# Down projections and the passage into the mixer of a trunk layer: the order of weight rounding, transposes and form sums

## The chip, the core and the metric

The kernel runs on one core of a Trainium2 chip. It is timed in device microseconds (us); the time before is 853.84 us, the median of three runs (853.50 to 854.26).

## What is computed

One layer of a decoder trunk, 512 tokens of width 1024, all in float32: a SwiGLU feed-forward network (FFN) of width 2816, a token mixer (pooling and sliding-window attention), and a second FFN, each between two RMS norms.

```python
def swiglu(h, w_gu, w_down):
    gate, up = jnp.split(h @ w_gu, 2, axis=-1)
    return (jax.nn.silu(gate) * up) @ w_down
...
h = swiglu(rms_norm(x, ffn1_pre[l]), ffn1_w_gu[l], ffn1_w_down[l])
x = x + 0.5 * rms_norm(h, ffn1_post[l])
h = token_mixer(rms_norm(x, mix_pre[l]), cos, sin, w_in[l], ...)
x = x + rms_norm(h, mix_post[l])
h = swiglu(rms_norm(x, ffn2_pre[l]), ffn2_w_gu[l], ffn2_w_down[l])
x = x + 0.5 * rms_norm(h, ffn2_post[l])
```

## The kernel before

**Matmuls in three.** A float32 product is made of three matmuls of a rounded kind: each operand is split into a high part (`hi`, rounded by a copy on ACT, L166 for weights, L630 for forms) and a low part (`lo`, the rest, a subtraction on DVE, L169 and L631). `mm3` (L356) issues hi by hi, hi by lo and lo by hi (L359 to L361).

**Weights.** The class `Weights` (L122) holds one list of weight tiles in the order of their use. `get(name, ahead)` makes all of them up to `ahead` beyond the one asked for (3 by default), `more(n)` the next n. For each one `make_to` (L153) issues loads on SP's queue, the rounding on ACT and the low part, on DVE or, where `W.lo` says so, on GpSimd (POOL). Six buffers of each part go round (WB), so the rounding of a tile waits until PE has used the tile six places before it, and a load waits until the low part of the tile whose raw buffer it takes is made. The order of rows on PE, DVE, ACT and POOL is the order of the code inside `in_order()`.

**The down projection** (`down_proj`, L611, once for each FFN) is a 2x2 block product of seven products, in the order 1, 5, 6, 3, 7, 2, 4. The 11 chunks of the hidden width go in pairs: weight tiles are named `d` with product and pair, so `f1_d70` to `f1_d75` are those of product 7 in the first FFN; the last, with one chunk, is half as wide. A pair is 12 matmuls, the last 6. The other operand is a *form* of the hidden activations (`form`, L617), three tiles for each product (`e70`, `e71`, `e72`), made during the product before it: products 5, 6, 3 and 7 first sum two tiles on DVE (L621 to L627), then ACT rounds and DVE makes the low part. Within a pair the weight is made first and the form behind it.

**Its end, and the passage.** When product 2 is over, `put_away(2)` (L665) adds it to what was kept. The tokens are four tiles of 128. Tiles 0 and 1 are complete then; tiles 2 and 3 are the two blocks that product 4 ends, one after the other (the tail: pairs 2 to 5, 21 matmuls for each block). For each tile ACT sums squares (`half_size`, L677), DVE applies the gain (`half_gain`, L686), `post_root` (L688) makes the mean square on DVE (L339) and its power on POOL (L334), and `add_to_x` (L691) updates x on DVE (L407). In the first FFN, steps of the mixer are woven into this by `then`: `size` (squares of x, L353), `root`, `norm` (xn, L378), `turn` (transposes on PE, L387; high parts xT on ACT, L393; low parts on DVE, L396) and `weights` (`weights1`, L906: the next tile of the mixer's input weights, wq0 to wq3, then wkv0, wkv1). The fourth of these and the first of wkv have their low part on POOL. PE then goes on in `mixer` (L1142) with `qkv_block(0)`: pq of tile 0 (24 matmuls of 512 columns), `turn1(2)`, pkv (24 of 256 columns), and a small transpose `pcols` before pq of tile 1. `root1(2)`, `norm1(2)`, `add_to_x(3)` and the rest of tiles 2 and 3 stand at the mixer's head.

Of the kernel before, what the change touches and what calls it, by code (L numbers as in the profile page):

```python
# [10 lines left out]
F32 = mybir.dt.float32  # L11
# [34 lines left out]
AHEAD = 3  # L46
# [21 lines left out]
def trunk_layer(  # L68
# [53 lines left out]
    class Weights:  # L122
# [25 lines left out]
        def split(self, name, shape):  # L148
            hi = wp.tile(list(shape), F32R, tag="hi", name=f"{name}_hi")
            lo = wp.tile(list(shape), F32R, tag="lo", name=f"{name}_lo")  # L150
            return hi, lo

        def make_to(self, n):  # L153
            while self.made < min(n, len(self.todo)):
                name, need, make, into = self.todo[self.made]
                self.load_to(need + self.run_ahead)
                src = make()
                if into is None:
                    hi, lo = self.split(name, src.shape)
                else:  # L160
                    whole, shape, at = into
                    if whole not in self.open:
                        self.open[whole] = self.split(whole, shape)
                    hi, lo = (part[at] for part in self.open[whole])
                if self.hi is nc.scalar:
                    nc.scalar.copy(hi, src)  # L166
                else:
                    nc.vector.tensor_copy(hi, src)
                self.lo.tensor_tensor(lo, src, hi.bitcast(F32), ALU.subtract)  # L169
                self.parts[name] = (hi, lo)  # L170
                self.made += 1

        def more(self, n):
            self.make_to(self.made + n)
# [436 lines left out]
    def down_proj(name, hs, ends, g_post, steps):  # L611
# [4 lines left out]

        def form(i, g):  # L617

            a11, a21, a12, a22 = (hs[g][:, f] for f in range(4))
            if i == 5:  # L620
                nc.vector.tensor_tensor(a21, a22, a21, ALU.subtract)  # L621
            elif i == 6:
                nc.vector.scalar_tensor_tensor(a11, a21, -1.0, a11, ALU.mult, ALU.subtract)  # L623
            elif i == 3:
                nc.vector.scalar_tensor_tensor(a21, a11, -1.0, a12, ALU.mult, ALU.subtract)  # L625
            elif i == 7:
                nc.vector.scalar_tensor_tensor(a11, a11, -1.0, a22, ALU.mult, ALU.subtract)  # L627
            src = {1: a11, 5: a21, 6: a11, 3: a21, 7: a11, 2: a12, 4: a22}[i]
            hi, lo = act_pair(f"{name}e{i}{g}", src.shape)
            nc.scalar.copy(hi, src)  # L630
            nc.vector.tensor_tensor(lo, src, hi.bitcast(F32), ALU.subtract)  # L631
            forms[i, g] = hi, lo
# [16 lines left out]
        def put_away(i):  # L649

            if i in (1, 5):
                kept[i] = wk.tile([P, 2, 512], F32, tag="sg2", bufs=2, name=f"{name}_p{i}")
                for t in range(2):
                    nc.scalar.copy(kept[i][:, t], into[i][t])
            elif i == 6:
                kept[i] = [slots_of["pool"].tile([P, 512], F32, tag="k", bufs=2, name=f"{name}_p6{t}") for t in range(2)]
                for t in range(2):
                    nc.scalar.copy(kept[i][t], xs_[t])
            for t in range(2):
                if i == 3:  # L660
                    nc.vector.scalar_tensor_tensor(kept[6][t], ys[t], -1.0, kept[6][t], ALU.mult, ALU.subtract)
                elif i == 7:
                    nc.vector.scalar_tensor_tensor(kept[5][:, t], xs_[t], -1.0, kept[5][:, t], ALU.mult, ALU.subtract)
                elif i == 2:
                    nc.vector.tensor_tensor(kept[1][:, t], zs_[t], kept[1][:, t], ALU.add)  # L665
# [28 lines left out]

        NW = (NCH + 1) // 2
        with behind(ends[0]):
            form(1, 0)
            form(1, 1)
        with behind(ends[1]):
            form(1, 2)  # L700
            W.get(f"{name}_d10")
        mix = steps if name == "f1" else {}

# [4 lines left out]
        with in_order():  # L708
            for at, i in enumerate(PRODUCTS[:-1]):
                for n in range(NW):  # L710
                    w = W.get(f"{name}_d{i}{n}")
                    if n % 2 == 0:
                        form(PRODUCTS[at + 1], n // 2)
                    multiply(i, n, w)
                    if n == 0 and at:
                        put_away(PRODUCTS[at - 1])
                    if i == 2 and 1 <= n <= 4:
                        half_size(n - 1, 1)
                        if n <= 2:
                            half_gain(n - 1, 1)  # L720
            i = PRODUCTS[-1]
            w = W.get(f"{name}_d{i}0")
            multiply(i, 0, w)
            put_away(2)
            for t in range(2):
                half_size(t, 0)
            for t in range(2):
                half_gain(t, 0)
                post_root(t)
            w = W.get(f"{name}_d{i}1")  # L730
            multiply(i, 1, w)
            for t in range(2):
                add_to_x(t)
                then("size", t)
            tail = [W.get(f"{name}_d{i}{n}", min(3, NW - 1 - n)) for n in range(2, NW)]
            then("root", 0)
            then("weights", 0)
            then("norm", 0)
            then("root", 1)
            then("weights", 1)  # L740
            then("norm", 1)
            for t in (2, 3):
                half_gain(t, 1)
            for n, w in enumerate(tail):
                multiply(i, n + 2, w, (0,))
            half_size(2, 0)
            half_gain(2, 0)
            post_root(2)
            for n, w in enumerate(tail):
                multiply(i, n + 2, w, (1,))  # L750
                if n == 1:
                    then("turn", 0)
                    then("weights", 2)
                    add_to_x(2)
# [82 lines left out]
    at = 0  # L837
# [65 lines left out]
            xT2.extend(act_pair(f"xT2_{i}") for i in range(4))  # L903
        transposes(t, xns[t], xT2, "mx")

    def weights1(n):  # L906
        W.run_ahead = 3
        W.lo = nc.gpsimd if n == 3 else nc.vector
        W.more(1)

    add_to_x = down_proj(
        "f1", hs, ends, g2,
        {"size": size1, "root": root1, "norm": norm1, "turn": turn1, "weights": weights1},
    )

    def project(ps, t, nm, per):
# [224 lines left out]

    def mixer():  # L1142
        with in_order():
            W.more(1)
            W.lo = nc.vector
            root1(2)
            norm1(2)
            add_to_x(3)
            W.more(1)
            size1(3)  # L1150
            qkv_block(0, lambda: turn1(2))
            root1(3)
            norm1(3)
# [232 lines left out]
```

## Time and profile before

| What | us |
|---|---|
| median of three runs | 853.84 |
| the profiled execution | 853.71 |
| its span on the core | 851.9 |
| mean granted TensorE clock over it | 0.989 of full |

The profile is of one execution. Engines: PE is TensorE (PEld its weight loads), DVE VectorE, ACT ScalarE, POOL GpSimd, SP the queue of loads. A row of a timeline has the start, the duration, the engine, the line, the operation, output and inputs, their shape and a count; in brackets stands how long the engine was idle ahead of it and what ended that. Names leave buffer numbers out, so `wq_lo` stands for the low part of any of the four. The view of waits has total time, number of times and longest. The granted clock is the share of full speed that TensorE was let run at.

### The profile page before, as it was taken

What the parts mean: (1) busy time and instruction counts of PE and PEld (TensorE: products, weight loads), DVE (VectorE), ACT (ScalarE), POOL (GpSimd) and SP (SyncE); (2) the same over time, 40 slices, a digit from 0 to 9 for tenths busy, and PEclk for the clock granted to TensorE, in tenths of its full rate; (3) what the DMA queues carried; (4) which work ended last, traced back from release to release, by engine and by line L of the source; (5) the groups of instructions that cost most, each with busy time, mean ns of one, the idle gap of its engine ahead of it and who ended that gap; (6) DMA issues with size and microseconds to landing.
All of it is one profiled execution on the core that took longest, in us unless ns stands there. A gap on an engine that the chain in (4) does not pass through costs nothing. (4 is left out here: it accounts for less than half of the span.)

```text
span 851.9 us, 14057 instructions
## 1 busy us (share of the span) xinstructions
PE 822.5 (97%) x5525; PEld 751.8 (88%) x5525; DVE 661.0 (78%) x854; ACT 467.5 (55%) x743; POOL 213.2 (25%) x293
## 2 busy tenths in 40 slices
PE   7999999999999999799999998999999999999996
PEld 5999999999988878688878878999999999888785
DVE  6987777777887799654666679777877778877895
ACT  6644445544555575535896567444444445555661
POOL 3103344433300001333532011133333344300001
PEclk9999999999999999989999999999999999999998
DMA  9428889988885567412005402268899888955542
GB/s 304 131 92 223 222 227 241 243 224 238 232 263 176 184 193 236 142 40 59 25 26 149 143 31 75 76 202 230 222 230 237 239 222 227 268 187 183 177 159 98
DMA packets 96877, 150.77 MB, mean 177 GB/s; under 512 B 6948, under 2 KB 53676, under 8 KB 96812
## 3 DMA queue, kind: packets, MB, share of 16 engines
q1 hardware_dynamic: 77100, 103.74, 38.0%
q0 software_dynamic: 19712, 46.15, 23.1%
q8 instruction: 43, 0.70, 0.3%
q14 instruction: 22, 0.18, 0.1%
HBM read 147.77 MB, written 48.23 MB: 230 GB/s over the span
## 5 line engine op out<-in xcount | busy, mean ns | idle before, releaser
L566 POOL DMA_DIRECT2D f_t<-in_ffn_w_down x132 | 89.6, 756 | 83.6 <-issue 50.7
L169 DVE TENSOR_TENSOR f_d_lo<-f_d_raw,f_d_hi 128x1024 fp32r<-128x1024 f32 x84 | 92.2, 1131 | 9.3 <-ACT f_d_hi L166 9.3
L166 ACT CAST f_d_hi<-f_d_raw 128x1024 fp32r<-128x1024 f32 x84 | 78.8, 977 | 6.9 <-PE f_z L361 6.7
L563 POOL COPY f_k<-f_h 1x1 f32<-1x1 f32 x18 | 21.0, 1166 | 130.8 <-DVE f_h L555 130.8
L590 ACT COPY f_h<-f_y 128x512 f32<-128x512 f32 x20 | 11.8, 588 | 76.1 <-PE f_y L361 75.5
L598 ACT ACTIVATE f_s<-f_s 128x1024 f32<-128x1024 f32 x20 | 21.2, 1061 | 41.5 <-DVE f_s L597 41.5
L566 POOL DMA_DIRECT2D f_t<-f_t x44 | 32.2, 795 | 36.6 <-issue 29.8
L630 ACT CAST f2e_hi<-f_h 128x1024 fp32r<-128x1024 f32 (+1 forms) x21 | 20.4, 977 | 30.9 <-DVE f_h L627 7.7
L630 ACT CAST f1e_hi<-f_h 128x1024 fp32r<-128x1024 f32 (+1 forms) x21 | 20.4, 977 | 30.7 <-DVE f_h L627 7.7
L595 ACT COPY f_s<-f_x 128x512 f32<-128x512 f32 x20 | 11.7, 587 | 46.3 <-PE f_x L361 46.3
L360 PE MATMUL f_x<-f_d_lo,f1e_hi 128*128 128x512 f32 x88 | 34.4, 390 | 0.8 <-DVE f_d_lo L169 0.8
L360 PE MATMUL f_x<-f_d_lo,f2e_hi 128*128 128x512 f32 x88 | 34.3, 390 | 0.8 <-DVE f_d_lo L169 0.8
L359 PE MATMUL f_x<-f_d_hi,f1e_hi 128*128 128x512 f32 x88 | 34.5, 392 | 0.7 <-DVE f_h L606 0.7
L359 PE MATMUL f_x<-f_d_hi,f2e_hi 128*128 128x512 f32 x88 | 34.4, 391 | 0.7 <-DVE f_h L606 0.7
L361 PE MATMUL f_x<-f_d_hi,f1e_lo 128*128 128x512 f32 x88 | 34.3, 389 | 0.0
L361 PE MATMUL f_x<-f_d_hi,f2e_lo 128*128 128x512 f32 x88 | 34.2, 389 | 0.0
L582 ACT COPY f_s<-f_x 128x512 f32<-128x512 f32 x20 | 11.7, 587 | 39.9 <-PE f_x L361 29.8
L631 DVE TENSOR_TENSOR f2e_lo<-f_h,f2e_hi 128x1024 fp32r<-128x1024 f32 (+1 forms) x21 | 23.6, 1133 | 11.4 <-ACT f2e_hi L630 11.4
L631 DVE TENSOR_TENSOR f1e_lo<-f_h,f1e_hi 128x1024 fp32r<-128x1024 f32 (+1 forms) x21 | 23.6, 1132 | 11.4 <-ACT f1e_hi L630 11.4
L334 POOL TENSOR_TENSOR r_f1po<-ms_f1po,half 128x1 f32<-128x1 f32 x4 | 3.5, 881 | 105.8 <-DVE ms_f1po L339 100.2
L334 POOL TENSOR_TENSOR r_f2po<-ms_f2po,half 128x1 f32<-128x1 f32 x4 | 3.5, 883 | 105.4 <-DVE ms_f2po L339 105.4
L359 PE MATMUL po<-wo_hi,yT_hi 128*128 128x512 f32 x64 | 25.3, 395 | 0.0
(1029 smaller groups left out, 3421.7 us busy)
## 6 DMA issues: line engine op xcount, KB each, us to landing
f_t<-in_ffn_w_down POOLq DMA_DIRECT2D x132, 256.0 KB, 6.3
f_d_raw<-f_t SPq DMA_DIRECT2D x40, 512.0 KB, 4.5
f_d_raw<-in_ffn_w_down SPq DMA_DIRECT2D x30, 512.0 KB, 4.4
f_t<-f_t POOLq DMA_DIRECT2D x44, 256.0 KB, 6.5
f_raw<-in_ffn_w_gu SPq DMA_DIRECT2D x8, 512.0 KB, 8.2
x<-in_x SPq DMA_DIRECT2D x4, 512.0 KB, 8.5
f_d_raw<-f_t SPq DMA_DIRECT2D x8, 256.0 KB, 3.7
wq_raw<-in_w_in SPq DMA_DIRECT2D x4, 512.0 KB, 4.2
```

The source lines that it names most:

```text
L166: nc.scalar.copy(hi, src)
L169: self.lo.tensor_tensor(lo, src, hi.bitcast(F32), ALU.subtract)
L359: nc.tensor.matmul(ps, wh, xh, start=first, stop=False, skip_group_check=open_)
L360: nc.tensor.matmul(ps, wh, xlo, start=False, stop=False, skip_group_check=open_)
L361: nc.tensor.matmul(ps, wlo, xh, start=False, stop=last, skip_group_check=open_)
L563: then = nc.gpsimd.tensor_copy(tick, hs[(c - 1) // 4][:1, 0, (c - 1) % 4, :1]).ins
L566: nc.gpsimd.dma_start(to, part, accum_op=op, max_dma_last_dim=2048)
L582: on_act.append(nc.scalar.copy(sg[:, :, a], px[:, :, a]).ins)
L590: on_act.append(nc.scalar.copy(h[1], py[:, :, a]).ins)
L598: on_act.append(nc.scalar.activation(sg, sg, AF.Silu, scale=-1.0).ins)
L630: nc.scalar.copy(hi, src)
L631: nc.vector.tensor_tensor(lo, src, hi.bitcast(F32), ALU.subtract)
```

## The change

`make_to` is cut in two: `begin` issues loads and the high part and returns what issues the low part. With it:
- the six input weights of the mixer are begun and ended at two places of the passage (`begin`, `low`), and all low parts are on DVE;
- the last product's weights are made earlier (`ahead` of 4 instead of 3 from the end of product 2 on, in both FFNs);
- both transposes of tiles 0 and 1 stand between the pairs of the tail's second block, at pairs 2 and 3; before, tile 0's stood behind pair 3 and tile 1's behind the block;
- the sums of squares of tile 2's x come behind the tail, the mean square of tiles 2 and 3 ahead of their gain (both FFNs);
- a form's sum stands ahead of the weight made in the same pair, its rounding and low part behind it (both FFNs).

```diff
+        def begin(self):
+            name, need, make, into = self.todo[self.made]
...
+            engine = self.lo
+            self.parts[name] = (hi, lo)
+            self.made += 1
+            return lambda: engine.tensor_tensor(lo, src, hi.bitcast(F32), ALU.subtract)
+
         def make_to(self, n):
             while self.made < min(n, len(self.todo)):
...
+                self.begin()()
...
             hi, lo = act_pair(f"{name}e{i}{g}", src.shape)
+            yield
             nc.scalar.copy(hi, src)
...
-                    w = W.get(f"{name}_d{i}{n}")
-                    if n % 2 == 0:
-                        form(PRODUCTS[at + 1], n // 2)
+                    half = form(PRODUCTS[at + 1], n // 2) if n % 2 == 0 else iter(())
+                    next(half, None)
+                    w = W.get(f"{name}_d{i}{n}", 4 if i == 2 and n == NW - 1 else AHEAD)
+                    next(half, None)
...
-            w = W.get(f"{name}_d{i}0")
+            w = W.get(f"{name}_d{i}0", 4)
             multiply(i, 0, w)
             put_away(2)
+            w = W.get(f"{name}_d{i}1", 4)
...
-            for t in range(2):
-                add_to_x(t)
-                then("size", t)
-            tail = [W.get(f"{name}_d{i}{n}", min(3, NW - 1 - n)) for n in range(2, NW)]
+            tail = [W.get(f"{name}_d{i}{n}", 0) for n in range(2, NW)]
+            then("begin", 0)
+            add_to_x(0)
+            then("size", 0)
+            add_to_x(1)
+            then("low", 0)
+            then("size", 1)
+            then("begin", 1)
             then("root", 0)
-            then("weights", 0)
+            half_gain(2, 1)
             then("norm", 0)
             then("root", 1)
-            then("weights", 1)
+            then("low", 1)
             then("norm", 1)
-            for t in (2, 3):
-                half_gain(t, 1)
+            half_gain(3, 1)
             for n, w in enumerate(tail):
                 multiply(i, n + 2, w, (0,))
             half_size(2, 0)
+            post_root(2)
             half_gain(2, 0)
-            post_root(2)
             for n, w in enumerate(tail):
                 multiply(i, n + 2, w, (1,))
+                if n == 0:
+                    then("begin", 2)
+                    then("low", 2)
+                    then("turn", 0)
                 if n == 1:
-                    then("turn", 0)
-                    then("weights", 2)
+                    then("begin", 3)
+                    then("low", 3)
                     add_to_x(2)
-                    then("size", 2)
+                    then("turn", 1)
+            then("begin", 4)
             half_size(3, 0)
+            then("size", 2)
+            then("low", 4)
+            post_root(3)
             half_gain(3, 0)
-            post_root(3)
-            then("turn", 1)
-            then("weights", 3)
...
-        W.lo = nc.gpsimd if n == 3 else nc.vector
-        W.more(1)
+        lows[n] = W.begin()
...
     def mixer():
         with in_order():
+            root1(2)
             W.more(1)
-            W.lo = nc.vector
-            root1(2)
             norm1(2)
             add_to_x(3)
-            W.more(1)
             size1(3)
```

Three places in the order of instructions. The first is DVE in the first FFN, during product 3, where the sums of product 7's forms (`h4`, `h8`: hidden activations) and the low parts of the weights stand. Before:

```order
L169 TENSOR_TENSOR f1_d34_lo_3347<-f1_d34_raw_3305,f1_d34_hi_3346 128x1024
L169 TENSOR_TENSOR f1_d35_lo_3365<-f1_d35_raw_3317,f1_d35_hi_3364 128x512
L627 SCALAR_TENSOR_TENSOR f1_h4_550<-f1_h4_550 128x1024
L631 TENSOR_TENSOR f1e71_lo_3370<-f1_h4_550,f1e71_hi_3369 128x1024
L169 TENSOR_TENSOR f1_d70_lo_3388<-f1_d70_raw_3344,f1_d70_hi_3387 128x1024
```

Now, from the sum on:

```order
L633 SCALAR_TENSOR_TENSOR f1_h4_550<-f1_h4_550 128x1024
L172 TENSOR_TENSOR f1_d35_lo_3368<-f1_d35_raw_3320,f1_d35_hi_3367 128x512
L638 TENSOR_TENSOR f1e71_lo_3364<-f1_h4_550,f1e71_hi_3363 128x1024
L172 TENSOR_TENSOR f1_d70_lo_3388<-f1_d70_raw_3344,f1_d70_hi_3387 128x1024
L633 SCALAR_TENSOR_TENSOR f1_h8_551<-f1_h8_551 128x768
```

The sum has gone ahead of one weight's low part; the form's own low part stays where it was.

The second is DVE in the passage, from the mean square of tile 0's x (`ms_b0`) to the norm of tile 2 (`xn_b2`); `f1_n2`, `f1_n3` and `f1_p5` are gains of tiles 2 and 3. Before, from tile 2's x on:

```order
L169 TENSOR_TENSOR wq2_lo_3852<-wq2_raw_3756,wq2_hi_3851 128x1024
L407 SCALAR_TENSOR_TENSOR x2_90<-f1_n2_3805,r_f1po2_3809,x2_90 128x512
L407 SCALAR_TENSOR_TENSOR x2_90<-f1_p5_3220,r_f1po2_3809,x2_90 128x512
L686 TENSOR_TENSOR f1_n3_3873<-f1_x1_2944,g2_2907 128x512
L339 SCALAR_TENSOR_TENSOR ms_f1po3_3875<-f1_sso_2945 128x1
L339 SCALAR_TENSOR_TENSOR ms_b2_3949<-ss2_b2_3857 128x1
L396 TENSOR_TENSOR xT2_0_lo_3824<-tr_mx10_3879,xT2_0_hi_3823 128x2x128
L396 TENSOR_TENSOR xT2_1_lo_3826<-tr_mx10_3879,xT2_1_hi_3825 128x2x128
L396 TENSOR_TENSOR xT2_2_lo_3828<-tr_mx11_3888,xT2_2_hi_3827 128x2x128
L396 TENSOR_TENSOR xT2_3_lo_3830<-tr_mx11_3888,xT2_3_hi_3829 128x2x128
L378 SCALAR_TENSOR_TENSOR xn_b2_3953<-x2_90,r_b2_3951,g3_2909 128x512 x2
```

Now, from the low part of wq3 on:

```order
L172 TENSOR_TENSOR wq3_lo_3858<-wq3_raw_3740,wq3_hi_3857 128x1024
L412 SCALAR_TENSOR_TENSOR x2_90<-f1_n2_3809,r_f1po2_3807,x2_90 128x512
L412 SCALAR_TENSOR_TENSOR x2_90<-f1_p5_3220,r_f1po2_3807,x2_90 128x512
L401 TENSOR_TENSOR xT2_0_lo_3824<-tr_mx10_3863,xT2_0_hi_3823 128x2x128
L401 TENSOR_TENSOR xT2_1_lo_3826<-tr_mx10_3863,xT2_1_hi_3825 128x2x128
L401 TENSOR_TENSOR xT2_2_lo_3828<-tr_mx11_3872,xT2_2_hi_3827 128x2x128
L401 TENSOR_TENSOR xT2_3_lo_3830<-tr_mx11_3872,xT2_3_hi_3829 128x2x128
L172 TENSOR_TENSOR wkv0_lo_3893<-wkv0_raw_3760,wkv0_hi_3892 128x1024
L344 SCALAR_TENSOR_TENSOR ms_f1po3_3903<-f1_sso_2945 128x1
L693 TENSOR_TENSOR f1_n3_3907<-f1_x1_2944,g2_2907 128x512
L344 SCALAR_TENSOR_TENSOR ms_b2_3949<-ss2_b2_3897 128x1
L172 TENSOR_TENSOR wkv1_lo_3956<-wkv1_raw_3817,wkv1_hi_3955 128x1024
```

Three low parts of weights (wq3, wkv0, wkv1) now stand on DVE ahead of `xn_b2`; before, none of them did, two of them being on POOL.

The third is PE in the tail's second block (`f1_x1`). Before, the last rows ahead of pq:

```order
L361 MATMUL f1_x1_2944<-f1_d43_hi_3682,f1e41_lo_3606 128x512
L387 MATMUL tr_mx00_3831<-ident_101,xn_b0_3764 128x128 x4
L387 MATMUL tr_mx01_3840<-ident_101,xn_b0_3764 128x128 x4
L359 MATMUL f1_x1_2944<-f1_d44_hi_3716,f1e42_hi_3650 128x512
L360 MATMUL f1_x1_2944<-f1_d44_lo_3717,f1e42_hi_3650 128x512
```

Now:

```order
L366 MATMUL f1_x1_2944<-f1_d42_hi_3670,f1e41_lo_3600 128x512
L392 MATMUL tr_mx00_3831<-ident_101,xn_b0_3770 128x128 x4
L392 MATMUL tr_mx01_3840<-ident_101,xn_b0_3770 128x128 x4
L364 MATMUL f1_x1_2944<-f1_d43_hi_3676,f1e41_hi_3599 128x512
L365 MATMUL f1_x1_2944<-f1_d43_lo_3677,f1e41_hi_3599 128x512
```

Tile 0's transposes have moved up by the six matmuls of pair 3; tile 1's, which before stood right ahead of pq, follow behind those six.

More of the change, by code (lines that the diff above doesn't have):

```diff
@@ L151, in split @@
             return hi, lo
+        def begin(self):
+            name, need, make, into = self.todo[self.made]
+            self.load_to(need + self.run_ahead)
+            src = make()
+            if into is None:
+                hi, lo = self.split(name, src.shape)
+            else:
+                whole, shape, at = into
+                if whole not in self.open:
+                    self.open[whole] = self.split(whole, shape)
+                hi, lo = (part[at] for part in self.open[whole])
+            if self.hi is nc.scalar:
+                nc.scalar.copy(hi, src)
+            else:
+                nc.vector.tensor_copy(hi, src)
+            engine = self.lo
+            self.parts[name] = (hi, lo)
+            self.made += 1
+            return lambda: engine.tensor_tensor(lo, src, hi.bitcast(F32), ALU.subtract)
         def make_to(self, n):
             while self.made < min(n, len(self.todo)):
[L155 to L171, printed above, removed]
+                self.begin()()
         def more(self, n):
@@ L696, in down_proj @@
         with behind(ends[0]):
-            form(1, 0)
-            form(1, 1)
+            for g in range(2):
+                list(form(1, g))
         with behind(ends[1]):
-            form(1, 2)
+            list(form(1, 2))
             W.get(f"{name}_d10")
@@ L729, in down_proj @@
                 post_root(t)
-            w = W.get(f"{name}_d{i}1")
             multiply(i, 1, w)
-            for t in range(2):
-                add_to_x(t)
-                then("size", t)
-            tail = [W.get(f"{name}_d{i}{n}", min(3, NW - 1 - n)) for n in range(2, NW)]
+            tail = [W.get(f"{name}_d{i}{n}", 0) for n in range(2, NW)]
[6 more added lines that the diff above has]
+            then("begin", 1)
             then("root", 0)
-            then("weights", 0)
+            half_gain(2, 1)
             then("norm", 0)
             then("root", 1)
-            then("weights", 1)
+            then("low", 1)
             then("norm", 1)
-            for t in (2, 3):
-                half_gain(t, 1)
+            half_gain(3, 1)
             for n, w in enumerate(tail):
@@ L904, in turn1, with begin1 @@
         transposes(t, xns[t], xT2, "mx")
-    def weights1(n):
+    lows = {}
+    def begin1(n):
         W.run_ahead = 3
-        W.lo = nc.gpsimd if n == 3 else nc.vector
-        W.more(1)
+        lows[n] = W.begin()
     add_to_x = down_proj(
         "f1", hs, ends, g2,
-        {"size": size1, "root": root1, "norm": norm1, "turn": turn1, "weights": weights1},
+        {"size": size1, "root": root1, "norm": norm1, "turn": turn1, "begin": begin1, "low": lambda n: lows[n]()},
     )
```

## The prediction

> **What bounds the kernel now.** I read the busy times first, then TensorE's waits by releaser, then the timeline of each engine round the longest of them, and last the granted clock there. This is the page's first part, busy us and share of the span:
>
> ```profile
> PE 822.5 (97%) x5525; PEld 751.8 (88%) x5525; DVE 661.0 (78%) x854; ACT 467.5 (55%) x743; POOL 213.2 (25%) x293
> ```
>
> TensorE (PE) is the bound, and the change leaves its instructions as many as they were. So only two things can be gained: time in which PE waits, and time in which its clock is low. The waits (us in total, times, longest) that lie where the change reaches:
>
> ```profile
> PE pq L359 <- ACT wq_hi L166: 3.2, 1, 3.2
> PE pq L360 <- POOL wq_lo L169: 1.9, 1, 1.9
> PE f_x L360 <- DVE f_d_lo L169: 1.7, 2, 0.8
> ...
> PE pt L1040 <- DVE st L1029: 1.0, 1, 1.0
> ```
>
> The first two lie in the passage from the first FFN to the mixer, the third once in each down projection; the last is the only one in the mixer behind the passage. PE's timeline of the passage (start, duration, what; in brackets the idle time ahead of a row):
>
> ```profile
> 346.80 1.03 PE L387 MATMUL tr_mx<-ident,xn_b 128*128 128x128 f32 x8
> 347.59 0.48 PE L359 MATMUL f_x<-f_d_hi,f1e_hi 128*128 128x512 f32 x1
> ...
> 354.48 0.39 PE L361 MATMUL pq<-wq_hi,xT_lo 128*128 128x512 f32 x1
> 358.07 0.50 PE L359 MATMUL pq<-wq_hi,xT_hi 128*128 128x512 f32 x1 [3.20 <-ACT wq_hi L166]
> 360.50 0.79 PE L360 MATMUL pq<-wq_lo,xT_hi 128*128 128x512 f32 x1 [1.93 <-POOL wq_lo L169]
> ...
> 364.12 1.97 PE L387 MATMUL tr_mx<-ident,xn_b 128*128 128x128 f32 x8 [1.12 <-DVE xn_b L378]
> ...
> 370.06 0.28 PE L359 MATMUL pkv<-wkv_hi,xT_hi 128*128 128x256 f32 x1
> 370.18 0.28 PE L360 MATMUL pkv<-wkv_lo,xT_hi 128*128 128x256 f32 x1
> ...
> 370.51 0.23 PE L1158 MATMUL pcols<-ident,rows 12*128 12x12 f32 x1
> ```
>
> Starts of 512-column matmuls stand 0.227 us apart where nothing waits, eight transposes take 0.79 (346.80 to 347.59), 256-column matmuls 0.12 (370.06 to 370.18). Between 354.71 (354.48 and 0.227) and 370.51 lie 6 of the first, 8 transposes and 24 of the last: 1.36 + 0.79 + 2.9 = 5.1 us of work in 15.8. So 10.7 us are lost, and the waits are only 6.3 of them. The rest is the clock. Stages of the trace with PE's busy time, granted clock, DMA share:
>
> ```profile
> 356.02:359.43 3.41, 0.50 (x1) 1.00 0.39 113
> 359.43:362.84 3.41, 2.34 (x5) 0.50 0.44 120
> ...
> 366.26:369.67 3.41, 3.41 (x18) 0.50 0.01 2
> 844.12:847.53 3.41, 0.84 (x4) 1.00 0.41 153
> ```
>
> The clock goes in steps of 3.41 us. After a step with one matmul it halves at 359.43, stays there through the half-filled step, and is back at 369.67, after the first full one. The step from 844.12, with 0.84 us busy, is followed by half clock too.
>
> **The form sums ahead of the low parts.** DVE, ACT and PE where product 7 of the first FFN begins:
>
> ```profile
> 299.32 1.22 DVE L627 SCALAR_TENSOR_TENSOR f_h<-f_h 128x1024 f32<-128x1024 f32 x1
> 301.66 1.23 DVE L631 TENSOR_TENSOR f1e_lo<-f_h,f1e_hi 128x1024 fp32r<-128x1024 f32 x1 [1.12 <-ACT f1e_hi L630]
> 302.80 1.22 DVE L169 TENSOR_TENSOR f_d_lo<-f_d_raw,f_d_hi 128x1024 fp32r<-128x1024 f32 x1
> ```
> ```profile
> 300.58 1.05 ACT L630 CAST f1e_hi<-f_h 128x1024 fp32r<-128x1024 f32 x1 [2.51 <-DVE f_h L627]
> ```
> ```profile
> 302.85 0.40 PE L359 MATMUL f_x<-f_d_hi,f1e_hi 128*128 128x512 f32 x1
> 304.07 0.50 PE L360 MATMUL f_x<-f_d_lo,f1e_hi 128*128 128x512 f32 x1 [0.83 <-DVE f_d_lo L169]
> ```
>
> DVE sums a form (1.14 us from start to start), ACT rounds it, DVE waits 1.12 for that, makes the form's low part, and only then the low part that PE wants at 304.07. With the sum first, DVE sums while ACT rounds the weights, and makes the weights' low part while ACT rounds the form. Up to product 7 each FFN has 10 sums that are moved so, about 1 us each, and DVE is ahead by far more than the 0.83 that was short. What is late next is the release of weight buffers, which is PE's own pace. The loss is 304.07 - 302.85 - 0.227 = 1.0, and about 0.1 in the next spacing; twice, **2.2 us**. Bounds: 0 if the load of that weight is what is late, 2.2 if all goes.
>
> **The end.** The root now precedes the gain. DVE and POOL after the last matmul:
>
> ```profile
> 845.78 0.69 DVE L686 TENSOR_TENSOR f_n<-f_x,g 128x512 f32<-128x512 f32 x1 [1.86 <-ACT j_f2po L677]
> 846.39 0.15 DVE L339 SCALAR_TENSOR_TENSOR ms_f2po<-f_sso 128x1 f32<-128x1 f32 x1
> 847.27 0.75 DVE L407 SCALAR_TENSOR_TENSOR x<-f_n,r_f2po,x 128x512 f32<-128x512 f32 x1 [0.73 <-POOL r_f2po L334]
> ```
>
> The mean square would start at 845.78 instead of 846.39, and the gain (0.61 to the next start) runs beside POOL's power: **0.6 us**, nothing behind it on DVE but the last sums.
>
> **The passage.** What sets its end in before: ACT's rounding of wq3 stands behind sums of squares that wait for x(2), POOL makes two low parts, and the root of tile 2 queues behind these.
>
> ```profile
> 330.00 1.06 ACT L166 CAST f_d_hi<-f_d_raw 128x1024 fp32r<-128x1024 f32 x1 [1.66 <-PE f_z L361]
> ...
> 353.79 0.63 ACT L353 ACTIVATE j_b<-x 128x512 bf16<-128x512 f32 x1 [4.21 <-DVE x L407]
> ```
> ```profile
> 345.86 1.40 POOL L334 TENSOR_TENSOR r_b<-ms_b,half 128x1 f32<-128x1 f32 x1 [2.26 <-DVE ms_b L339]
> ...
> 358.10 2.35 POOL L169 TENSOR_TENSOR wq_lo<-wq_raw,wq_hi 128x1024 fp32r<-128x1024 f32 x1 [0.62 <-ACT wq_hi L166]
> ...
> 362.73 0.55 POOL L334 TENSOR_TENSOR r_b<-ms_b,half 128x1 f32<-128x1 f32 x1
> ```
> ```profile
> 333.40 1.37 DVE L665 TENSOR_TENSOR f_p<-f_z,f_p 128x512 f32<-128x512 f32 x2 [0.72 <-PE f_z L361]
> ...
> 345.63 1.22 DVE L169 TENSOR_TENSOR wq_lo<-wq_raw,wq_hi 128x1024 fp32r<-128x1024 f32 x1
> ...
> 350.50 1.41 DVE L396 TENSOR_TENSOR xT_lo<-tr_mx,xT_hi 128x256 fp32r<-128x256 f32 x4
> ...
> 352.95 0.74 DVE L407 SCALAR_TENSOR_TENSOR x<-f_n,r_f1po,x 128x512 f32<-128x512 f32 x1
> ...
> 363.31 1.41 DVE L378 SCALAR_TENSOR_TENSOR xn_b<-x,r_b,g 128x512 f32<-128x512 f32 x2 [5.14 <-POOL r_b L334]
> ```
>
> Now DVE carries all of it in one queue, which I add up in before's clock times. A low part costs 1.14 from start to start (301.66 to 302.80), a half of xn 0.67 (1.41 for two, of which the second takes the 0.74 of a half), and so a half of x; a gain 0.61, a mean square 0.1, the four xT_lo 1.4. A root that POOL starts under a DVE operation on SBUF ends 0.5 after it (345.86: 1.40 instead of 0.55, to 0.5 behind the low part of 345.63).
> - d44's low part stands ahead of the product sums. Its high part waits for the buffer of d24, one weight tile (12 matmuls, 2.72) after the one released at 330.00: 332.7; ACT 1.06, DVE 1.22: 335.0. So the sums of 333.40 start at **335.0**. Two sums 1.37, d45's low part 0.6, two gains and a mean square 1.3, the root 0.5, four halves of x 2.7: 341.5.
> - wq0's low part, mean square, gain, root 0.5: 343.8; xn(0) to 345.2. Its transposes, six matmuls ahead of 346.80, stand at 345.4 on PE: no wait. wq1, root 0.5, xn(1): 348.3. PE wants its second half at 348.0 (345.4, 0.79, six matmuls, 0.4): 0.3 of waiting. Gain, mean square, gain, wq2, then xT_lo(0) from 350.7 to 352.0; pq, which now would start at 350.9 (17 spacings ahead of 354.48, and the 0.3), has the first of these at 351.1: another 0.3 at most.
> - wq3, x(2): 354.5 (before: 354.4). xT_lo(1), wkv0, mean square, gain, mean square, wkv1: 358.8; root 0.5; first half of xn(2) there at 360.1. Before: 364.05.
> - PE would end pq at 354.71 + 1.36 = 356.1, with the two waits 356.6. It then **waits 3.6 us** for the transposes of tile 2, which before waited for POOL. They start at 360.2, take 0.28 (second half) and 0.79, then 2.9 of pkv: pcols at 364.1 instead of 370.51, 6.35. The same sum on before's order comes out 0.15 early: **6.2 us**.
>
> ACT's part hides in this: it rounds wq3 as soon as PE has used d43, no longer behind the sums of squares of 353.79. SP's loads of wkv and wu come no later, as their buffers are those of d44, d45 and wq0, whose low parts DVE makes earlier or 1 us later. POOL loses two operations of 2.35 and 2.3, and DVE's 1.14 each stand in the sum.
>
> The clock: from 356.6 to 361.3 PE has no matmul but transposes. On a grid of 3.41, some step keeps at most (6.83 - 4.7) / 2 = 1.1 us of matmuls, near the 0.84 that was followed by half clock and far from the 2.3 that keep neither. So I let it halve, until the first full step: 3.4 to 6 us of work at half clock cost 1.7 to 3.0, and I take 2.3. The passage gives 6.2 - 2.3 = **3.9 us**.
>
> **A rule against this forecast.** This step had nothing but transposes (columns: PE, PEld, DVE, ACT, POOL, clock):
>
> ```profile
> 7.86:11.27 3.41, 1.24 (x10) 0.84 (x8) 2.78 (x6) 1.67 (x4) 0.55 (x1) 1.00 1.04 356
> ```
>
> The clock was half in the step behind it. The Trainium skill, "TensorE: Matmul & The Clock Gate", Part 4: PE-mode transpose, says that transposes do not count as busy; by that rule, the trace agrees. The same page, Part 1: The HAM clock gate, lets the clock fall after an idle window of about 3.4 us; the step at 356.02, with a matmul in it, speaks against reading this as wholly idle. By that reading the sum would be the first rival's.
>
> **Sum.** 853.71 for the profiled execution (its median 853.84 is 0.02% above), less 2.2, 0.6 and 3.9: **847.0 us**. Its own range, from a clock cost of 1.7 to 3.4, the first term at 1.7, and 0.7 in the sum of DVE's queue: 845.7 to 848.7.
>
> **Rivals.**
> - The clock stays at full, since no step of the grid is wholly without matmuls: a whole one fits into 4.7 us in 1.3 / 3.41 of all positions. Against it: 356.02 and 844.12. 853.71 - 2.2 - 0.6 - 6.2 = 844.7.
> - The form sums change nothing, because d70's load or buffer is what is late, not DVE's queue. For it speaks only that a load is not seen in that row; 847.0 + 2.2 = 849.2.
> - DVE's queue, without a gap from 335 to 360, is longer: some 45 operations at 0.03 more, and a second half-filled step at half clock (1.7): 850.
> - The passage's gain is given back by a wait further on in the mixer, and the forms bring nothing: 853.1. Against it: PE's one wait of 1.0 in the mixer behind the passage is for its own chain.
> - Slower: a sum of 1.14 ahead of a low part delays PE wherever that low part has no lead. It decides from four such sums (4.5 / 1.14, the forms' 2.2 being lost then) of the 22 that are moved. If the 18 of products 6, 3 and 7 all do, 849.2 + 20.5 = 869.7. Against it: DVE idles 1.12 behind the sum in the rows above.
>
> **Chances.** Forecast 0.52, full clock 0.20, longer queue 0.12, forms without effect 0.10, given back 0.03, slower 0.03. A measurement of this kernel tells 0.2% (1.7 us) from no change: faster 0.94, within 0.03, slower 0.03. From 844.3 to 850.2 the range takes in all but the last two.
>
> **What would show it.** The wait of 0.83 before f_d_lo gone in both FFNs; wq_hi and wq_lo gone from PE's waits; instead one wait of 3 to 4 us of tr_mx for xn_b, with half clock for one or two steps behind it; POOL with roots alone until wpl; the last mean square ahead of the gain. A wait of tr_mx under 2.5 us, or a clock that stays full, makes it too slow a forecast; a new wait for f_d_lo or put_away, too fast.

## The result, and the profile after

| | before | after |
|---|---|---|
| median, us (4 runs each, in turns) | 854.05 | 843.98 |
| lowest and highest | 853.50, 854.31 | 843.83, 844.82 |
| profiled execution, us | 853.71 | 843.83 |
| its span, us | 851.9 | 841.9 |

The ratio is 0.9883, 95% interval 0.9871 to 0.9895. The forecast was 847.0 with a range from 844.3: faster, but by 3 us more than forecast.

First the engines, from the page of the changed kernel (busy us, share of the span, instructions). TensorE's matmuls are as many as before, its share is the same 97%; what went is waiting, and some half clock:

```profile
PE 819.0 (97%) x5525; PEld 750.6 (89%) x5525; DVE 662.7 (79%) x856; ACT 470.1 (56%) x743; POOL 207.8 (25%) x291
```

PE's waits in the changed kernel where the prediction spoke of them (us in total, times, longest):

```profile
PE tr_mx L392 <- DVE xn_b L383: 3.5, 1, 3.5
...
PE f_x L364 <- DVE f_h L611: 1.4, 2, 0.7
...
PE pt L1057 <- DVE st L1046: 1.0, 1, 1.0
```

The waits of pq for `wq_hi` and `wq_lo` are gone, and so are both of `f_x` for `f_d_lo`; the new one of `tr_mx` is there with 3.5 (3.6 forecast). But the view of before has one more line that no longer appears, and the prediction did not name it:

```profile
PE f_x L359 <- DVE f_s L534: 1.6, 1, 1.6
```

It lies in the second FFN, 170 us behind the passage, where the first product of a gate and up pair (`f2_x1`) begins. PE and DVE's last `f_s` there, first in before, then in the changed kernel:

```profile
533.86 0.64 PE L478 MATMUL f_c<-f2b_lo,f_c_hi 128*128 128x256 f32 x4
536.14 0.36 PE L359 MATMUL f_x<-f2b_hi,f_1p_hi 128*128 128x256 f32 x1 [1.64 <-DVE f_s L534]
...
535.31 0.68 DVE L534 SCALAR_TENSOR_TENSOR f_s<-f_c,f_s 128x512 f32<-128x512 f32 x1
```
```profile
527.61 0.64 PE L483 MATMUL f_c<-f2b_lo,f_c_hi 128*128 128x256 f32 x4
528.09 0.28 PE L364 MATMUL f_x<-f2b_hi,f_1p_hi 128*128 128x256 f32 x1
...
529.07 0.67 DVE L539 SCALAR_TENSOR_TENSOR f_s<-f_c,f_s 128x512 f32<-128x512 f32 x1
```

In the changed kernel PE starts `f2_x1` before that `f_s`, in before behind it.

The passage in the changed kernel, PE's timeline and then DVE's:

```profile
344.35 1.03 PE L392 MATMUL tr_mx<-ident,xn_b 128*128 128x128 f32 x8
...
346.61 1.03 PE L392 MATMUL tr_mx<-ident,xn_b 128*128 128x128 f32 x8
...
354.76 0.39 PE L366 MATMUL pq<-wq_hi,xT_lo 128*128 128x512 f32 x1
358.69 1.58 PE L392 MATMUL tr_mx<-ident,xn_b 128*128 128x128 f32 x8 [3.54 <-DVE xn_b L383]
359.92 0.56 PE L364 MATMUL pkv<-wkv_hi,xT_hi 128*128 128x256 f32 x1
...
364.33 0.23 PE L1173 MATMUL pcols<-ident,rows 12*128 12x12 f32 x1
```
```profile
333.85 1.28 DVE L672 TENSOR_TENSOR f_p<-f_z,f_p 128x512 f32<-128x512 f32 x2
...
353.03 1.41 DVE L401 TENSOR_TENSOR xT_lo<-tr_mx,xT_hi 128x256 fp32r<-128x256 f32 x4
354.36 1.22 DVE L172 TENSOR_TENSOR wkv_lo<-wkv_raw,wkv_hi 128x1024 fp32r<-128x1024 f32 x1
...
356.22 1.22 DVE L172 TENSOR_TENSOR wkv_lo<-wkv_raw,wkv_hi 128x1024 fp32r<-128x1024 f32 x1
357.88 1.41 DVE L383 SCALAR_TENSOR_TENSOR xn_b<-x,r_b,g 128x512 f32<-128x512 f32 x2 [0.44 <-POOL r_b L339]
```

PE runs through both transposes and all of pq without a stop, then waits for DVE, whose queue is never idle for more than 0.44 from 333.85 to the norm of tile 2 at 357.88. The clock there, in stages with PE's busy time and the granted clock behind the engines' busy times:

```profile
352.78:356.19 3.41, 2.37 (x11) 1.63 (x9) 3.41 (x9) 1.21 (x4) 0.41 (x1) 1.00 0.40 154
356.19:359.60 3.41, 0.91 (x6) 0.67 (x7) 2.97 (x6) 0.00 (x0) 1.54 (x2) 1.00 0.51 154
359.60:363.02 3.42, 3.42 (x18) 3.42 (x17) 1.95 (x5) 2.94 (x10) 0.00 (x0) 0.50 0.01 2
```

One step of 3.41 us has no matmul but 0.91 us of transposes; the next one is at half clock, and full again behind it.

**Where the 10 us are.** Whole times carry a scatter that has nothing to do with the change: the first matmul of the first down projection starts anywhere from 241.4 to 243.6 in the fourteen traces of this case, though nothing ahead of it differs. So I cut each trace at five starts on PE and compare the stretches. In the changed kernel the first, the second and the fourth of these are:

```profile
242.03 0.40 PE L364 MATMUL f_x<-f_d_hi,f1e_hi 128*128 128x512 f32 x1
...
397.58 0.38 PE L1057 MATMUL pt<-ident,st 128*128 128x128 f32 x2
...
729.69 0.40 PE L364 MATMUL f_x<-f_d_hi,f2e_hi 128*128 128x512 f32 x1
```

The third is the `f_x` at 528.09 above, the fifth the last matmul (835.17). In before they start at 241.83, 403.78, 536.14, 737.79 and 844.58. Stretch A, from the first to the second, holds the first down projection, the passage and qkv; B the rest of the mixer up to `f2_x1`; C the second gate and up; D the second down projection; E the end. The differences of the starts, for all kernels that were run (us):

| kernel | A | B | C | D | E | bank of `f2_c11` |
|---|---|---|---|---|---|---|
| before | 161.95 | 132.36 | 201.65 | 106.79 | 7.35 | 1 |
| after | 155.55 | 130.51 | 201.60 | 105.48 | 6.73 | 5 |
| b_forms | 159.97 | 132.32 | 201.66 | 105.51 | 7.34 | 1 |
| b_turn1 | 162.24 | 130.60 | 201.60 | 106.80 | 7.34 | 6 |
| b_end | 161.83 | 132.33 | 201.67 | 106.84 | 6.75 | 1 |
| b_nopool | 159.48 | 132.33 | 201.66 | 106.80 | 7.35 | 1 |
| a_oldforms | 156.81 | 132.38 | 201.66 | 106.84 | 6.74 | 1 |
| a_turns_back | 155.49 | 130.48 | 201.60 | 105.48 | 6.74 | 5 |
| a_ahead_back | 153.24 | 132.35 | 201.66 | 105.49 | 6.75 | 1 |
| a_fill | 154.11 | 134.13 | 201.66 | 105.49 | 6.74 | 0 |
| a_pool | 156.25 | 132.31 | 201.66 | 105.51 | 6.74 | 1 |
| a_pool_early | 156.52 | 130.50 | 201.60 | 105.49 | 6.75 | 5 |
| a_norm_first | 153.03 | 133.22 | 201.66 | 105.50 | 6.74 | 1 |
| a_both_lows_late | 152.02 | 130.48 | 201.60 | 105.49 | 6.73 | 5 |

After against before: A 6.40 less, B 1.85, D 1.31, E 0.62, together 10.2; the changed kernel's first start is 0.2 later, so its span is 10.0 shorter. The last column is read from the built programs and is the key to B. PSUM, the memory into which TensorE writes its sums, is handed out by the kernel as eight banks or as four pairs of them: `f2_c11` is the fourth of the four gate and up tiles that stand ahead of `f2_x1`, and `f2_x1` takes PSUM banks 0 and 1 in every one of these programs.

### The profile page after: what moved, and what is told of

Its sections match the earlier page's. It is cut to its first block, busy times and chain, and to the rows that moved or that the text cites. A ratio compares the mean times of both kernels' runs of the same rounds, so it can differ in the third digit from the quotient of the medians.

```text
span 841.9 us, 14062 instructions
## 1 busy us (share of the span) xinstructions
PE 819.0 (97%) x5525; PEld 750.6 (89%) x5525; DVE 662.7 (79%) x856; ACT 470.1 (56%) x743; POOL 207.8 (25%) x291
## 5 line engine op out<-in xcount | busy, mean ns | idle before, releaser
L172 DVE TENSOR_TENSOR f_d_lo<-f_d_raw,f_d_hi 128x1024 fp32r<-128x1024 f32 x84 | 94.8, 1131 | 25.3 <-ACT f_d_hi L166 25.3
```

The lines of the kernel that those rows point to most:

```text
L172: return lambda: engine.tensor_tensor(lo, src, hi.bitcast(F32), ALU.subtract)
```

## The experiments

Names with b_ are the kernel before with one thing changed, names with a_ the changed kernel.

**b_forms: the form sums alone.**

```diff
             hi, lo = act_pair(f"{name}e{i}{g}", src.shape)
+            yield
...
-                    w = W.get(f"{name}_d{i}{n}")
-                    if n % 2 == 0:
-                        form(PRODUCTS[at + 1], n // 2)
+                    half = form(PRODUCTS[at + 1], n // 2) if n % 2 == 0 else iter(())
+                    next(half, None)
+                    w = W.get(f"{name}_d{i}{n}")
+                    next(half, None)
```


> The kernel before with the form sums moved and nothing else. If the forms' term holds: both waits of 0.8 us of f_x for f_d_lo gone, 2.2 us off, 851.8 us. If the release of weight buffers is what is late there: 854.0, with a wait of f_x for something else in their place. In both cases the wait of 1.6 us of f_x for f_s in the second FFN stays, since the last gate and up block (f2_c11) still has PSUM bank 1 there; if the form sums are what removed that wait, 850.0.

851.46 us against 853.71 beside it, ratio 0.9971 (0.9959 to 0.9982). Both waits for `f_d_lo` are gone, D is 1.28 less, and the wait for `f_s` stays. A is 1.98 less: 1.27 of it up to the last matmul of the first down projection, the rest in the passage, whose wait for `wq_lo` is 1.6 there in place of 1.9 and whose three steps of half clock end earlier in pkv. The release of weight buffers does not hold these places.

**b_turn1: one statement written earlier, for its bank.**

```diff
-            post_root(3)
             then("turn", 1)
+            post_root(3)
```


> The kernel before with the transposes of tile 1 written one statement earlier, ahead of tile 3's mean square; PE's order is the same, and in the built program f2_c11 comes to bank 6 instead of bank 1, which lies under the pair f2_x1. Theory of the bank: the wait of 1.6 us for f_s goes though nothing else changes, 1.8 us off, 852.1 us, and the passage takes what it took. Theory that the wait went because DVE reaches that place earlier in the changed kernel: the wait stays at 1.6, 853.9 us.

852.74 against 853.71, ratio 0.9990 (0.9981 to 0.9999). PE's order is the same instruction by instruction, except that the built program has one wait less, the one right ahead of `f2_x1`. A is 0.3 longer, which was not expected: on DVE the low parts of tile 1's xT now stand ahead of two mean squares, and the wait for `wq_lo` is 2.6 in place of 1.9. B falls by 1.76: the wait for `f_s` is gone. PE and DVE in this run:

```profile
534.32 0.28 PE L359 MATMUL f_x<-f2b_hi,f_1p_hi 128*128 128x256 f32 x1
```
```profile
535.28 0.68 DVE L534 SCALAR_TENSOR_TENSOR f_s<-f_c,f_s 128x512 f32<-128x512 f32 x1
```

DVE does its last `f_s` at the same place as in before (535.31), and PE no longer waits for it: that operation reads `f2_c11`, which is in bank 6 here and so not under `f2_x1`.

**a_oldforms: the changed kernel without the moved sums.**

```diff
-                    next(half, None)
                     w = W.get(f"{name}_d{i}{n}", 4 if i == 2 and n == NW - 1 else AHEAD)
-                    next(half, None)
+                    list(half)
```


> The changed kernel with each form's sum behind the weight's low part again. The two waits for f_d_lo come back (2.2 us). Theory of the bank: the built program has f2_c11 in bank 1 again, so the wait for f_s comes back too (1.85 us): 848.0 us. Theory of the passage (what DVE does there sets it): the wait stays away, 846.2 us.

848.69, ratio 0.9941 (0.9929 to 0.9953), against 0.9883 of the changed kernel. A and D are longer by 1.26 and 1.36, and B by 1.87, with the wait back although the passage is that of the changed kernel:

```profile
531.76 0.36 PE L364 MATMUL f_x<-f2b_hi,f_1p_hi 128*128 128x256 f32 x1 [1.64 <-DVE f_s L539]
```

So neither the forms nor the passage remove it as such; the bank does. In the table B is 130.5 or 130.6 in all five kernels with bank 5 or 6, and 132.3 or more in all nine with bank 0 or 1. The built programs also show where the bank is decided. The changed kernel and a_oldforms agree in every PSUM tile's bank up to the end of the mixer, and so do before and b_turn1 with each other. There `po111` and `po110`, two sums of the mixer's output projection, come to each other's banks, and `f2_c11` gets the bank that `po110` had. In the five kernels with bank 5 or 6 `po111` has bank 1; in the other nine it does not.

**b_end: the mean square ahead of the gain, second FFN only.**

```diff
             half_size(3, 0)
-            half_gain(3, 0)
+            if mix:
+                half_gain(3, 0)
             post_root(3)
+            if not mix:
+                half_gain(3, 0)
```
(and the same for tile 2.)


> The kernel before with the mean square of tiles 2 and 3 ahead of their gain in the second FFN only. If the end's term holds: 0.6 us less from the last matmul to the end, 853.4 us. If the root there waits for something else, 854.0.

853.53 against 853.71, ratio 0.9998 (0.9989 to 1.0007): as a whole time it can't be told from nothing. In the trace E is 0.60 less, which is the term.

**a_fill: work for PE in its wait.**

```diff
         project(pq, t, "wq", 2)
+        if t == 0:
+            pkv, wh = bank(f"pkv{t}"), W.get("wq3", 0)[0]
+            for _ in range(14):
+                nc.tensor.matmul(pkv, xT2[0][0][:, 0, :P], wh[:, 0], start=True, stop=True)
         between()
-        pkv = bank(f"pkv{t}")
+        if t:
+            pkv = bank(f"pkv{t}")
```


> The changed kernel with 14 more matmuls of 512 columns on PE between pq and the transposes of tile 2 (3.2 us, inside the wait of 3.5; their product is overwritten). Theory that the half clock comes from the step without matmuls: the wait shrinks to 0.4, the clock stays full, and from the first pq to the first pt PE needs 46.4 us in place of 48.0. Rival, that the half clock has another cause (the transposes, or what follows them): 48.0 still. The built program has f2_c11 in bank 0 under f2_x1, so the wait for f_s comes back by the theory of the bank (1.85): 844.2 us with the first, 845.8 with the second.

845.92, ratio 0.9903 (0.9888 to 0.9917). No half clock in the passage, a wait of 0.4, and A is 1.44 less; from the first pq to the first pt 46.6 (349.71 to 396.30) in place of 48.0. Two steps of its clock at the place where the changed kernel had 0.91 us of work and then half clock:

```profile
356.86:360.27 3.41, 2.95 (x18) 2.12 (x17) 2.96 (x5) 0.04 (x1) 1.16 (x1) 1.00 0.49 150
360.27:363.68 3.41, 3.41 (x27) 3.21 (x27) 1.94 (x6) 3.38 (x11) 0.00 (x0) 1.00 0.01 2
```

The transposes of tile 2 start as late as in the changed kernel (116.7 behind the first start in both). So the half clock cost 1.4 to 1.5, and what makes it in this place is the step without matmuls. The total did not follow, since B grew by 3.62: the wait for `f_s` (1.0 here), and two steps at half clock that the changed kernel's trace does not have. The forecast of 844.2 had counted neither of these two steps. The stages around both:

```profile
431.94:435.36 3.42, 2.46 (x18) 2.11 (x18) 1.51 (x6) 2.89 (x8) 0.61 (x1) 1.00 0.02 5
435.36:438.77 3.41, 3.41 (x9) 2.62 (x8) 1.91 (x3) 3.35 (x8) 1.95 (x5) 0.50 0.00 0
513.87:517.28 3.41, 1.86 (x14) 1.46 (x13) 3.41 (x5) 1.39 (x4) 0.00 (x0) 1.00 0.22 75
517.28:520.69 3.41, 3.41 (x17) 3.41 (x18) 3.41 (x6) 2.37 (x5) 0.00 (x0) 0.50 0.15 38
```

The first is the place of the mixer's wait of 1.0 (`pt` for `st`). My reading, which no run tests by itself, is that shifting PE by a microsecond or two lets the 3.41 us grid cut its waits elsewhere.

**a_pool: the low parts of wq3 and wkv0 on GpSimd again.**

```diff
         W.run_ahead = 3
+        W.lo = nc.gpsimd if n in (3, 4) else nc.vector
         lows[n] = W.begin()
...
             root1(2)
+            W.lo = nc.vector
             W.more(1)
```


> The changed kernel with the low parts of wq3 and wkv0 on GpSimd again, at their new places. Theory that DVE's one queue sets the end of the passage now, and that GpSimd was late only because its inputs were: xn of tile 2 comes 2.3 us earlier, the wait of tr_mx falls from 3.5 to about 1.3, the clock may stay full (1.6), and GpSimd has both low parts done before 353; from the first pq to the first pt 44.2 to 45.8 us instead of 48.0. Rival, that low parts on GpSimd are themselves what held the passage: a wait of pq for wq_lo of 2 us or more comes back and the passage takes 48.0 or more. f2_c11 is in bank 1, so 1.85 us for f_s come back in both: 842.0 to 843.6 against 845.8 or more.

847.19, ratio 0.9918 (0.9901 to 0.9935). The theory was wrong, and the rival right in the time alone (48.7 us from the first pq to the first pt): no wait for `wq_lo` came back, but xn of tile 2 came no earlier, and the wait of `tr_mx` grew to 4.2. DVE and POOL in this run:

```profile
351.97 1.59 DVE L412 SCALAR_TENSOR_TENSOR x<-f_n,r_f1po,x 128x512 f32<-128x512 f32 x1
353.48 2.88 DVE L412 SCALAR_TENSOR_TENSOR x<-f_p,r_f1po,x 128x512 f32<-128x512 f32 x1
```
```profile
349.65 3.36 POOL L172 TENSOR_TENSOR wq_lo<-wq_raw,wq_hi 128x1024 fp32r<-128x1024 f32 x1
352.95 2.86 POOL L172 TENSOR_TENSOR wkv_lo<-wkv_raw,wkv_hi 128x1024 fp32r<-128x1024 f32 x1
```

A half of x takes 0.74 elsewhere, and 2.88 beside GpSimd's subtraction, which itself is stretched from 2.35 to 2.86 and 3.36. The Trainium skill, "SBUF — State Buffer", section "SBUF: two separate sides", says that a DVE operation with two inputs in SBUF and a GpSimd operation that reads SBUF take a shared port pair as a lock for a whole instruction, so that one waits for the other; these rows agree: DVE's 2.88 end 0.55 behind GpSimd's second subtraction. In before GpSimd's two low parts stood in a stretch where DVE idled for 5.14; there they took 2.35 and slowed no DVE operation, though PE waited for the first of them.

**a_pool_early: both wkv low parts on GpSimd, right behind their high parts.**

```diff
             then("begin", 4)
+            then("low", 4)
             half_size(3, 0)
+            then("begin", 5)
+            then("low", 5)
             then("size", 2)
-            then("low", 4)
+            then("root", 2)
```
(with `W.lo` on GpSimd for these two, and `add_to_x(3)` and `size1(3)` behind `turn1(2)`.)


> The changed kernel with both wkv low parts on GpSimd, right behind their high parts (GpSimd idles there), and tile 2's root behind them. By the theory of DVE's queue: GpSimd ends both by 355, tile 2's norm starts at 355.7 instead of 357.9, the wait of tr_mx is 1 to 1.5, the clock stays full, 3.5 us off; f2_c11 is in bank 5, so no wait for f_s: 840.4 us. Rival, that GpSimd's work under DVE's is slowed so that the root comes as late as now: 844 or more.

845.29, ratio 0.9900 (0.9885 to 0.9914), slower than the changed kernel: A 156.52, a wait of 4.9. DVE's rows under the two GpSimd subtractions:

```profile
350.81 3.11 DVE L172 TENSOR_TENSOR wq_lo<-wq_raw,wq_hi 128x1024 fp32r<-128x1024 f32 x1
353.84 2.86 DVE L412 SCALAR_TENSOR_TENSOR x<-f_n,r_f1po,x 128x512 f32<-128x512 f32 x1
```

The rival was right in time, but what was slowed most was DVE: 2.3 us of it were handed to GpSimd, and it lost 4.0 on two operations (3.11 and 2.86 in place of 1.22 and 0.74).

**b_nopool: the same low parts on DVE, in the order of before.**

```diff
-        W.lo = nc.gpsimd if n == 3 else nc.vector
```


> The kernel before with the low parts of wq3 and the first wkv on DVE at their old places, and nothing else. f2_c11 is in bank 1, so the wait for f_s stays. If GpSimd was what held the passage: the wait of pq for wq_lo falls from 1.9 to 0.7, tr_mx no longer waits, 2.5 us off, 851.4 us. If DVE's own chain holds it as much: 853.9. The rest of the passage's gain is then that of the earlier rounding of wq3.

852.15 against 853.47, ratio 0.9980 (0.9970 to 0.9989). The whole time fell by 1.3 (0.9 to 2.6 by the interval), A by 2.47. That is the 2.5 expected, but in other parts: the wait for `wq_lo` fell to 0.8, that of `tr_mx` did not go but is 0.7, and the clock was at half for two steps instead of three. The waits give 1.6, which leaves 0.85 for the clock. The wait of 3.2 for `wq_hi` is left. So with the order of before, GpSimd's two low parts cost 2.5; with the new order a_pool has two of them back for 0.7 in A. What GpSimd costs depends on the order, so the passage's 5.1 can't be split by this run alone.

**a_turns_back: both transposes at their old places.**

```diff
                     then("low", 2)
-                    then("turn", 0)
                 if n == 1:
+                    then("turn", 0)
                     then("begin", 3)
                     then("low", 3)
                     add_to_x(2)
-                    then("turn", 1)
+            then("turn", 1)
```


> The changed kernel with the transposes of tiles 0 and 1 at their old places (behind pair 3 of the last block, and behind the block). f2_c11 is in bank 5. Theory of DVE's queue: PE reaches the end of pq later by less than the 3.5 us that it waits for tile 2 anyway, and DVE's order is the same: 844.0 us, with a shorter wait of tr_mx. Rival, that the earlier transposes themselves are a gain of one or two times 0.79: 844.8 to 845.6.

843.52, ratio 0.9884 (0.9866 to 0.9901), and A 155.49 against 155.55. Moving the transposes into the tail brings nothing by itself: PE reaches its wait for tile 2 in either case. That wait is 3.6, not shorter as expected.

**a_ahead_back: the last product's weights as late as before.**

```diff
-                    w = W.get(f"{name}_d{i}{n}", 4 if i == 2 and n == NW - 1 else AHEAD)
+                    w = W.get(f"{name}_d{i}{n}")
...
-            w = W.get(f"{name}_d{i}0", 4)
+            w = W.get(f"{name}_d{i}0")
...
-            w = W.get(f"{name}_d{i}1", 4)
+            w = W.get(f"{name}_d{i}1")
...
-            tail = [W.get(f"{name}_d{i}{n}", 0) for n in range(2, NW)]
+            tail = [W.get(f"{name}_d{i}{n}", min(3, NW - 1 - n)) for n in range(2, NW)]
```


> The changed kernel with the last product's weights made as late as before (three ahead, the last two in one piece). f2_c11 is in bank 1, so 1.85 us for f_s come back. Theory that the wait for d44's rounding stands in DVE's one queue: the product sums start about 1.2 us earlier, all behind them too, 844.6 us. Rival, that only the order on DVE changes and not its end: 845.8. Rival, that the earlier weights are needed: PE waits for a low part of d43 to d45, 847 or more.

844.61, ratio 0.9900 (0.9879 to 0.9921), with the wait for `f_s` back. But for that wait the kernel would be ahead of the changed one: A is 2.3 less. The norm of tile 2 comes 0.8 earlier, the wait of `tr_mx` is 2.8 instead of 3.5, and in the profiled execution the clock then stayed full. So this part of the change costs some 0.8, and in that execution the half clock too. That the median meets the expected 844.6 is luck: 0.8 came in place of 1.2, and the four executions lie between 843.04, the profiled one, and 846.32.

**a_norm_first: tile 2's norm ahead of the wkv low parts.**

```diff
-            then("low", 4)
+            then("root", 2)
...
-            root1(2)
-            W.more(1)
+            begin1(5)
             norm1(2)
-            add_to_x(3)
-            size1(3)
-            qkv_block(0, lambda: turn1(2))
+            lows[4]()
+            qkv_block(0, lambda: (turn1(2), lows[5](), add_to_x(3), size1(3)))
```


> The changed kernel with root and norm of tile 2 ahead of the low parts of wkv0 and wkv1 on DVE (the second of these behind tile 2's xT). Theory that these 2.3 us of DVE are what tr_mx waits for: its wait falls from 3.5 to about 1, the clock stays full, pkv then ends some 2.5 us earlier, held by the second low part. Rival, that the wait only moves on to pkv: 48.0 us from the first pq to the first pt, as now. f2_c11 is in bank 1 (1.85 us back): 843.3 us against 845.8.

843.59, ratio 0.9879 (0.9865 to 0.9894). PE's waits:

```profile
PE f_x L364 <- DVE f_s L539: 1.6, 1, 1.6
...
PE pkv L365 <- DVE wkv_lo L172: 1.1, 2, 0.8
...
PE tr_mx L392 <- DVE xn_b L383: 0.9, 1, 0.9
```

A is 2.5 less, as expected. B is 2.7 more: 1.85 for the bank, and 0.9 at a step of half clock at the mixer's wait for `st`, the one that a_fill met.

**a_both_lows_late: the same in another order, with another bank.**

(The lines are set against a_norm_first.)

```diff
             begin1(5)
             norm1(2)
             lows[4]()
-            qkv_block(0, lambda: (turn1(2), lows[5](), add_to_x(3), size1(3)))
+            lows[5]()
+            qkv_block(0, lambda: (turn1(2), add_to_x(3), size1(3)))
```


> The changed kernel with root and norm of tile 2 ahead of both wkv low parts, and tile 3's x behind tile 2's xT. Its DVE order up to pkv costs what that of the run before with the norm first cost (45.5 us from the first pq to the first pt, against 48.0), and f2_c11 is in bank 5. If bank and norm are two separate gains: no wait for f_s, 1.85 us under that run, 841.7 us. If what was gained at the norm is lost where PE goes on (half clock in a later step of the mixer, a wait for the later tile 3): 843 to 844.

840.85 us, ratio 0.9849 (0.9834 to 0.9865): the fastest kernel of the study, 3 us under the changed one. So bank and norm are two separate gains. From the first pq to the first pt it takes 44.5, 1.0 less than expected. A is 152.02, B 130.48, and from 40 us to the last matmul the clock is full throughout. PE's waits in the passage:

```profile
PE tr_mx L392 <- DVE xn_b L383: 0.9, 1, 0.9
PE pkv L365 <- DVE wkv_lo L172: 0.4, 1, 0.4
```

## Why the prediction was wrong

- **Forms, 2.2 forecast: 2.6 measured.** The mechanism was right (both waits gone in b_forms, back in a_oldforms). The term counted 1.0 of lateness and 0.1 of the next spacing from one row; a stretch of the whole projection gives 1.26 to 1.36 for each FFN.
- **End, 0.6: 0.60 and 0.62.** Right.
- **Passage, 3.9: 5.1** (A's 6.40 less 1.3 for the forms). The steps held: DVE's single queue, the product sums behind d44's low part, no wait for `wq_hi` or `wq_lo`, a wait of 3.54 for 3.6, half clock behind it. Two sizes were off. The clock was entered with 2.3, and a_fill shows 1.44: it was half for one step alone, and full again at 363.02. And DVE's queue ended 0.4 earlier than summed: the transposes of tile 2 were put at 360.2, 118.4 behind the first start of before, and came at 358.69 - 242.03 + 1.3 (the forms') = 118.0.
- **The step that failed: a term of 1.85, in stretch B, put at nothing.** The prediction's sum ended with three terms and took all between passage and second down projection as untouched; PE's wait of 1.6 for `f_s` was not even among the waits that it listed. b_turn1 and a_oldforms show what removed it: `f2_c11` came to bank 5 instead of 1, so that `f2_x1` no longer lies over the tile that DVE reads last. The bank is decided at the end of the mixer, where `po111` and `po110` change places. What in the new order makes the builder change them is open: a_oldforms has the passage of the changed kernel and does not have it. This step, and not a rival, is why the time fell under the range: with the 1.85 the profiled execution would have taken 845.7. The range had bounds for every cost that was seen, and none for a place that the change reaches only through the allocation. With the later start, 0.4 + 1.2 + 1.85 - 0.2 = 3.25 is the distance from 847.0 to the profiled 843.83, within 0.1. (A slip without effect: if the three parts of the prediction's own range are added, its upper end is 847.0 + 1.1 + 0.5 + 0.7 = 849.3 and not 848.7. The miss lies on the other side.)
- **The rivals.** Full clock: its 844.7 lies nearest to the measured time, but by luck, since the clock was at half in the profiled execution; a_ahead_back shows how near full clock was. The Trainium skill, "TensorE: Matmul & The Clock Gate", Part 1: The HAM clock gate, wants an idle window, and its Part 4: PE-mode transpose, does not count transposes as busy in the same way; the step at 356.19 held 0.91 us of transposes alone, so it is idle by that rule, and the trace agrees. The clock also fell behind the step at 513.87 of a_fill, which held 1.86 us of matmuls, so an idle window does not tell all of it. Forms without effect, a longer queue, the gain given back in the mixer, and a delay by the sums: none of them came.
- **What the change owes to which of its parts.** Form sums 2.6, the passage 5.1, the end 0.6, the bank 1.85. Within the passage GpSimd is worth 2.5 by the order of before (b_nopool) and 0.7 by the new one (a_pool). That the earlier rounding of wq3 gives most of the rest is argued and not shown: the wait of 3.2 for `wq_hi` is there in b_nopool and gone in the changed kernel. The transposes in the tail bring nothing (a_turns_back), and the weights made earlier cost 0.8 (a_ahead_back).

What is open: the split of the passage beyond these, since it was not tried to round wq3 earlier by itself, and why `po111` and `po110` change places.

## What to carry to other kernels

Where the builder, and not the code, chooses the buffers, list the tiles of a later stage that lie over each other, before and after: an edit can add or remove a wait hundreds of microseconds behind it. After a wait has moved to another engine, look at what stands in that engine's queue ahead of the one operation that is waited for; here one tile's root and norm, put ahead of two low parts that PE wanted only later, took 3.5 us off stretch A, the half clock's 1.4 among them (a_both_lows_late). Compare stretches between fixed instructions rather than whole times, where starts and clock steps scatter by more than the effect.

## What the runs showed of the hardware

- DVE operations with two inputs in SBUF and GpSimd's subtractions did not run beside each other at their own pace: a row of 0.74 became 2.88 (a_pool), and one of 1.22 became 3.11 (a_pool_early).
- The half clock does not follow from PE's busy time in a step alone, nor from that without the transposes. It came behind steps with 0.91 us (the changed kernel), but also behind 1.86 and 2.46 (a_fill; 1.30 of the latter were transposes), and did not come behind these:

```profile
356.19:359.61 3.42, 1.98 (x16) 1.75 (x16) 2.92 (x5) 0.63 (x2) 0.59 (x1) 1.00 0.38 133
```
```profile
355.10:358.51 3.41, 2.16 (x16) 1.71 (x16) 3.36 (x7) 1.29 (x4) 0.58 (x2) 1.00 0.51 154
```

The first is a_ahead_back, the second a_norm_first, each with 1.07 us of transposes. So one and the same wait can cost a half-clock step in one kernel and none in another: the mixer's 1.0 for `st` did so in a_fill and a_norm_first, for 0.9 in the latter, and not in the changed kernel.
